# Which PSUM banks the 256-column projections of a two-layer trunk sum in

## The chip, the cores and the metric

The kernel runs on one core of one Trainium2 chip. The metric is the device time of one execution in microseconds (us). The core's engines are TensorE (PE in the profile; its weight loads stand apart as PEld), VectorE (DVE), ScalarE (ACT), GpSimd (POOL) and SyncE (SP, which here only issues DMAs). Every engine works through its own list of instructions in order, and the lists meet by semaphores. PSUM, where TensorE writes its sums, has eight banks of 128 partitions by 512 float32 values in this kernel's layout.

## The reference, cut to what matters

A sequence of 256 tokens of width 1024 passes two layers. Each layer has a mixer and an expert stage (PEER), and each of these ends in a residual sum and a layer norm.

```
proj = h @ w_in                       # one wide projection, split among three groups
y_a  = gelu(rg_gate) * rg_lru(conv(rg_x))            # recurrent group
y_b  = mamba2(z, silu(conv(xbc)), dt)                # state-space group, chunks of 128
y_c  = sliding_window_attention(q, k, v, sinks)      # attention group
mix  = concat(y_a, y_b, y_c) @ w_out
h    = layer_norm(alpha * h + mix)
q    = h @ wq;  scores = q . keys     # 8 heads, top 16 of 2 x 128 keys each
ffn  = sum over chosen experts of gate * gelu(h . u) * v
h    = layer_norm(alpha * h + ffn)
```

The matrix products keep float32 precision: each float32 operand is split into a high and a low part, and three products (high by high, high by low, low by high) are summed.

## The kernel before

**Weights.** All weight blocks (128 by 1024 float32) lie in one list (`items`) in the order of use. A DMA brings a block into one of four raw buffers. ScalarE copies it to `hi` (L119), and VectorE, or GpSimd for the numbers in `on_pool`, subtracts to get `lo` (L120). `hi` and `lo` have three buffers each, so the split of block n+3 waits until TensorE is done with block n. `weights(key)` (lines 123 to 128) asks for a block and starts the split of two more. In a layer's list, blocks 0 to 12 are xBC and dt, 13 to 16 the recurrent input (rgx), 17 to 20 its gate (rgg), 21 to 26 q, k and v; of 13 to 26, GpSimd splits 14, 16 and 18 and VectorE the rest.

**Two kinds of PSUM buffer.** The pool has two names with four banks each:

```
def bank(shape, name="w"):
    return psum.tile(shape, F32, name="w", bufs=4)

def acc_bank():
    return psum.tile([128, 512], F32, name="acc", bufs=4)
```

A tile of a name takes the next of its four buffers, and its first write waits until everything that read or wrote the tile before it in that buffer is done. `acc` serves the 512-column sums: the z projection (two at a time), the output projection (four), the expert stage's up products (one each for a pair of expert blocks) and its down products (four). `w` serves the rest: the transposes of the layer norm (L282), the background products of the mixer and of the routing, and the 256-column projections.

**The 256-column projections** go through `proj_T` (line 336): 24 matmuls of 128 by 128 by 256 columns into one `[128, 256]` tile, with a weight block as the stationary operand and the transposed residual stream `hTh`, `hTl` as the moving one. Each is then copied out by ScalarE (L745 and L761 into `xp`, L769 into `gg`, L777 into `qT`, `kT`, `vT`; L850 in the expert stage). A mixer has 27 of them (12 xBC, 1 dt, 4 rgx, 4 rgg, 6 qkv), an expert stage 8.

**Background work.** What the three groups compute beside the projections is written as generators, of which the mixer takes a step or two after each projection (`bg.step`). After the 12 xBC blocks these are, in the order written: a small product `pc` and transpose `pb` (L465, then mm through L194), four transpose groups `pt` of `xs` (L484), read by two VectorE operations each (L496 into `xdt`, L497 into `y`), the decay sums from `da` (into `odec`, L490), and then state products, gates (`bda`) and attention. Each of them takes `w` banks.

**Order.** Within a layer the order of each engine's list is fixed when the program is built: the framework's planner goes by the order in which the code emits the instructions, by what they need, and by its own estimate of when buffers come free. Only the layer norm (VectorE, ScalarE), the routing (VectorE) and short groups of matmuls have an order written out by hand. The output projection takes 16 blocks; block 4 is the first that needs the attention, block 8 the first that needs the state-space group.

Of the kernel before, what the change touches and what calls it, by code (L numbers as in the profile page):

```python
# [17 lines left out]
SEQ = 256  # L18
# [30 lines left out]
def trunk(ctx, tc, x, wst, ut, vr, pp_d, rb_d, lnrow, bd_d, keys_d, out):  # L49
# [76 lines left out]
    def weights(key, ahead=True):  # L126
        n = index[key]
        pump_split(n)
        if ahead:
            pump_split(n + LOOK)  # L130
        return splits.pop(n)
# [64 lines left out]
# [5 lines that stand above are left out]
# [135 lines left out]
    def proj_T(w, hT, ps, first=False):  # L336
        hi, lo = w
        hTh, hTl = hT
        if first:
            for n, (a, b) in enumerate(((hi, hTh), (lo, hTh), (hi, hTl))):  # L340
                for k in range(KD):
                    mm(ps, a[:, k * 128:(k + 1) * 128], b[:, k, :], n == 0 and k == 0, n == 2 and k == KD - 1)
            return
        for k in range(KD):
            s = slice(k * 128, (k + 1) * 128)
            mm(ps, hi[:, s], hTh[:, k, :], k == 0, False)
            mm(ps, hi[:, s], hTl[:, k, :], False, False)
            mm(ps, lo[:, s], hTh[:, k, :], False, k == KD - 1)
# [46 lines left out]
    def mixer(l, mix, h, hT, pre):  # L395
# [20 lines left out]
        def dt_task(ps):  # L416
            dtT = mix.tile([16, SEQ], F32, name="dtT")
            ACT.activation(dtT, ps[0:16, :], AF.Copy)
            pd = bank([128, 2, 16])
            for tb in range(2):  # L420
                PE.transpose(pd[:, tb, :], dtT[:, tb * 128:(tb + 1) * 128], ident[0:16, 0:16])
            yield
            DVE.tensor_tensor(dt, pd, RB("dtb", l)[:, None, :].to_broadcast([128, 2, 16]), op=OP.add)
            dr = mix.tile([128, 2, 16], F32, name="dt_raw")
            DVE.tensor_copy(dr, dt)
            log1p_exp_neg_abs(mix, dt.rearrange("p a b -> p (a b)"), dr.rearrange("p a b -> p (a b)"), 32, "sp")
            DVE.scalar_tensor_tensor(da, dt, -1.0, av[:, None, :].to_broadcast([128, 2, 16]),
                                     op0=OP.mult, op1=OP.mult)
            ACT.activation(das[:, 0], da, AF.Copy)
            DVE.tensor_tensor(das[:, 1], da, das[:, 0].bitcast(F32), op=OP.subtract)  # L430
            yield
            yield
# [16 lines left out]
        def ssm_conv(blk, xp):  # L449
            conv(xs[:, blk, :], xp, lambda i: P("scw", l, blk * 4 + i))  # L450
            ACT.activation(xs[:, blk, :], xs[:, blk, :], AF.Silu, bias=P("scb", l, blk))
            yield
# [145 lines left out]
        def rg_conv(blk, xp):  # L598
            conv(xc[:, blk, :], xp, lambda i: P("rgw", l, blk * 4 + i), P("rgb", l, blk))
            yield  # L600
# [138 lines left out]

        order = [8, 9, 10, 11, 0, 1, 2, 3, 4, 5, 6, 7]  # L740
        for n, blk in enumerate(order):
            ps = bank([128, SEQ])
            proj_T(weights(("w", l, n if n < 4 else n + 1)), hT, ps, n == 0)
            xp = pads[n % 4]
            ACT.activation(xp[:, 3:3 + SEQ], ps, AF.Copy)  # L745
            bg.add(ssm_conv(blk, xp))
            bg.step(1)
            if n == 3:
                ps = bank([128, SEQ])
                proj_T(weights(("w", l, 4)), hT, ps)  # L750
                dtt = dt_task(ps)
            if n == 4:
                next(dtt)
# [2 lines left out]
        bg.add(ssm_core())  # L756
        n0 = 1 + N_XBC
        for blk in range(4):
            ps = bank([128, SEQ])
            proj_T(weights(("w", l, n0 + blk)), hT, ps)  # L760
            ACT.activation(pads[blk][:, 3:3 + SEQ], ps, AF.Copy)  # L761
            for _ in rg_conv(blk, pads[blk]):
                pass
            bg.step(RX)
        n0 += N_RGX
        for blk in range(4):
            ps = bank([128, SEQ])
            proj_T(weights(("w", l, n0 + blk)), hT, ps)
            ACT.activation(gg[:, blk, :], ps, AF.Copy)  # L769
            bg.step(RA)  # L770
        n0 += N_RGG
        bg2.add(rg_core())
        for i in range(6):
            ps = bank([128, SEQ])
            proj_T(weights(("w", l, n0 + i)), hT, ps)
            dst = qT[:, i, :] if i < 4 else (kT if i == 4 else vT)
            ACT.activation(dst, ps, AF.Copy)  # L777
            bg.step(RA)
            bg2.step(RB2)
# [54 lines left out]
    def peer(l, pool, hT):  # L834
# [10 lines left out]

        qT = view(120, 8).rearrange("p (a b) -> p a b", b=SEQ)
        for hh in range(8):
            ps = bank([128, SEQ])
            proj_T(weights(("w", l, N_IN + N_OUT + hh)), hT, ps, hh == 0)
            ACT.activation(qT[:, hh, :], ps, AF.Copy)  # L850
        scs = [view(104 + 8 * tb, 8).rearrange("p (h i k) -> p h i k", i=2, k=128) for tb in range(2)]

        for tb in range(2):
            for hq in range(2):
                ps = [bank([128, 4, 128]) for _ in range(2)]
# [185 lines left out]
        for jp_ in range(64):  # L1041
            ps = psum.tile([128, 2, SEQ], F32, name="acc", bufs=4)
# [77 lines left out]
    for l in range(DEPTH):  # L1120
        po = mixer(l, mix, h, hT, consts.pop() if consts else None)

        def resid(tb, nh, acc, po=po, h=h):
            cs = slice(nh * 512, (nh + 1) * 512)
            DVE.scalar_tensor_tensor(h[:, tb, cs], h[:, tb, cs], ALPHA, po[tb][nh], op0=OP.mult, op1=OP.add,
                                     accum_out=acc)
        hT = layer_norm(h, mix, resid, (("g1", l), ("b1", l)), h_dram[l], ("w", l, N_IN + N_OUT))
        mixp.__exit__(None, None, None)
        with tc.tile_pool(name=f"peer{l}", bufs=1) as pool:
            po = peer(l, pool, hT)  # L1130
        mixp = tc.tile_pool(name=f"mix{l + 1}", bufs=1)
        mix = mixp.__enter__()
        h = mix.tile([128, 2, D], F32, name="h")

        def resid2(tb, nh, acc, po=po, h=h, l=l):
            cs = slice(nh * 512, (nh + 1) * 512)
            DVE.scalar_tensor_tensor(h[:, tb, cs], rawtile(("h", l, tb))[:, cs], ALPHA * GS, po[tb][nh],
                                     op0=OP.mult, op1=OP.add, accum_out=acc)
            if nh:
                rawdone(("h", l, tb))  # L1140
        last = l == DEPTH - 1
        outs = [out[tb * 128:(tb + 1) * 128, :] for tb in range(2)]
        hT = layer_norm(h, mix, resid2, (("g2", l), ("b2", l)), outs if last else None,
                        None if last else ("w", l + 1, 0), final=last, unit=GS)
# [74 lines left out]
```

## Time and profile before

| | |
|---|---|
| runs shown | 2021.58, 2026.04, 2031.02 us; median 2026.04 |
| profiled execution | 2025.82 us |
| its span in the trace | 2024.0 us |
| mean granted TensorE clock | 0.988 |
| PE busy | 1958.4 us, 97% of the span |
| DVE, ACT, POOL busy | 1471.8 (73%), 1050.0 (52%), 218.1 (11%) |

The span is the time between the first and the last instruction of the trace. Busy is the sum of an engine's instructions without overlaps. The granted clock is a share of TensorE's full 2.4 GHz; 0.50 means 1.2 GHz. The layers' stages by time: mixer of layer 0 from about 18 to 208 us, its expert stage to about 1010, mixer of layer 1 from about 1018 to 1208, its expert stage to about 2014.

### The profile page before, as it was taken

How to read it: one execution, taken by the hardware profiler on the slowest of the kernel's cores; microseconds unless marked ns; L12 is line 12 of the kernel's file. 1: busy time of each engine (PE TensorE's matmuls, PEld its weight loads, DVE VectorE, ACT ScalarE, POOL GpSimd, SP SyncE). 2: the span in 40 equal slices, each digit the busy share in tenths (PEclk: the TensorE clock that was granted, in tenths of full speed). 3: DMA queues.
4: the chain of work that ended last, by engine and by line, in shares of the span. 5: the costliest groups of instructions: out<-in, count | busy, mean ns of one | idle time of the engine just before them, and what ended most of it. 6: DMA issues, size and time to landing. Idle time of an engine off the chain costs nothing. (4 is left out here: it accounts for less than half of the span.)

```text
span 2024.0 us, 33680 instructions
## 1 busy us (share of the span) xinstructions
PE 1958.4 (97%) x13292; PEld 1774.9 (88%) x13292; DVE 1471.8 (73%) x2584; ACT 1050.0 (52%) x1531; POOL 218.1 (11%) x114
## 2 busy tenths in 40 slices
PE   6999899999999999999999999999999999999998
PEld 6887899999999888888788769989999998888886
DVE  8896598677888655555697865996788885555555
ACT  5576454554444544444566754545444444444444
POOL 3100155500000000000011002554000000000000
PEclk9999899999999999999999999999999999999999
DMA  6434454554444656656554245545445446665665
GB/s 208 136 115 156 167 178 157 169 165 157 158 163 160 187 191 195 196 190 196 194 186 134 96 156 181 177 142 176 158 157 164 159 158 191 194 197 188 197 195 169
DMA packets 95919, 344.85 MB, mean 170 GB/s; under 512 B 11680, under 2 KB 11952, under 8 KB 95760
## 3 DMA queue, kind: packets, MB, share of 16 engines
q1 hardware_dynamic: 95552, 342.27, 51.8%
q8 instruction: 104, 1.70, 0.3%
q0 software_dynamic: 208, 0.42, 0.1%
q14 instruction: 55, 0.45, 0.1%
HBM read 339.51 MB, written 3.15 MB: 169 GB/s over the span
## 5 line engine op out<-in xcount | busy, mean ns | idle before, releaser
L119 ACT ACTIVATE hi<-raw 128x1024 fp32r<-128x1024 f32 x630 | 664.5, 1057 | 565.8 <-PE acc L194 290.7
L120 DVE TENSOR_TENSOR lo<-raw,hi 128x1024 fp32r<-128x1024 f32 x550 | 688.5, 1252 | 318.0 <-ACT hi L119 317.9
L194 PE MATMUL acc<-hTh,hi 128*128 128x256 f32 x2048 | 592.7, 289 | 0.0
L194 PE MATMUL acc<-hTh,lo 128*128 128x256 f32 x2048 | 581.5, 284 | 9.8 <-DVE lo L120 6.1
L194 PE MATMUL acc<-hTl,hi 128*128 128x256 f32 x2048 | 580.9, 284 | 0.0
L194 PE MATMUL acc<-hi,hTl 128*128 128x512 f32 x1056 | 412.0, 390 | 0.0
L194 PE MATMUL acc<-lo,hTh 128*128 128x512 f32 x1056 | 411.6, 390 | 0.0
L194 PE MATMUL acc<-hi,hTh 128*128 128x512 f32 x1056 | 411.3, 390 | 0.0
L194 PEld LDWEIGHTS acc<-hTh,lo 128*128 128x128 f32 x2048 | 394.3, 193 | 11.4 <-DVE lo L120 6.7
L194 PEld LDWEIGHTS acc<-hTl,hi 128*128 128x128 f32 x2048 | 394.8, 193 | 0.0
L194 PEld LDWEIGHTS acc<-hTh,hi 128*128 128x128 f32 x2048 | 394.4, 193 | 0.2
L120 POOL TENSOR_TENSOR lo<-raw,hi 128x1024 fp32r<-128x1024 f32 x80 | 203.3, 2545 | 597.1 <-ACT hi L119 543.1
L194 PEld LDWEIGHTS acc<-hi,hTl 128*128 128x128 f32 x1056 | 198.2, 188 | 42.8 <-issue 1.6
L194 PEld LDWEIGHTS acc<-hi,hTh 128*128 128x128 f32 x1056 | 198.2, 188 | 41.7 <-issue 0.7
L194 PEld LDWEIGHTS acc<-lo,hTh 128*128 128x128 f32 x1056 | 198.3, 188 | 40.5
L194 PE MATMUL w<-hTh,hi 128*128 128x256 f32 x560 | 161.7, 299 | 7.6 <-DVE y L497 5.7
L1080 ACT ACTIVATE hTh<-act 128x512 fp32r<-128x512 f32 x124 | 81.1, 659 | 166.2 <-PE acc L194 166.2
L1081 DVE TENSOR_TENSOR hTl<-act,hTh 128x512 fp32r<-128x512 f32 x124 | 85.5, 693 | 100.4 <-ACT hTh L1080 100.4
L194 PE MATMUL w<-hTh,lo 128*128 128x256 f32 x560 | 156.7, 289 | 0.0
L194 PE MATMUL w<-hTl,hi 128*128 128x256 f32 x560 | 155.5, 287 | 0.0
L969 DVE TENSOR_TENSOR eq<-iota,ijT 128x1024 f16<-128x1024 f16 x128 | 88.4, 690 | 53.1 <-PE w L194 52.3
L194 PEld LDWEIGHTS w<-hTh,hi 128*128 128x128 f32 x560 | 109.9, 202 | 9.9 <-issue 6.2
(265 smaller groups left out, 1919.8 us busy)
## 6 DMA issues: line engine op xcount, KB each, us to landing
raw<-in_ut SPq DMA_DIRECT2D x256, 512.0 KB, 3.5
raw<-in_vr SPq DMA_DIRECT2D x256, 512.0 KB, 3.6
raw<-in_wst SPq DMA_DIRECT2D x118, 512.0 KB, 3.5
raw<-in_lnrow SPq DMA_DIRECT2D x8, 512.0 KB, 3.7
hd<-h SPq DMA_DIRECT2D x4, 512.0 KB, 3.9
raw<-hd SPq DMA_DIRECT2D x4, 512.0 KB, 4.2
h<-in_x SPq DMA_DIRECT2D x2, 512.0 KB, 5.7
y<-in_lnrow SPq DMA_DIRECT2D x2, 512.0 KB, 7.0
```

Of the source, the lines that this page charges most:

```text
L119: ACT.activation(hi, raw, AF.Copy)
L120: (POOL if n in on_pool else DVE).tensor_tensor(lo, raw, hi.bitcast(F32), op=OP.subtract)
L194: PE.matmul(ps, lhsT, rhs, start=start, stop=stop)
L969: DVE.tensor_tensor(eq.rearrange("p c a k e -> p (c a) k e"), iota2[:, None, :, :].to_broadcast(sh), pairs(ijT[:, g]), op=OP.is_equal)
L1080: ACT.activation(gh, src, AF.Copy)
L1081: DVE.tensor_tensor(gl, src, gh.bitcast(F32), op=OP.subtract)
```

## The change

Each of the 256-column projections takes an `acc` buffer and uses its first 256 columns. All else is as it was.

```diff
         for n, blk in enumerate(order):
-            ps = bank([128, SEQ])
+            ps = acc_bank()[:, 0:SEQ]
             proj_T(weights(("w", l, n if n < 4 else n + 1)), hT, ps, n == 0)
...
             if n == 3:
-                ps = bank([128, SEQ])
+                ps = acc_bank()[:, 0:SEQ]
                 proj_T(weights(("w", l, 4)), hT, ps)
...
         for blk in range(4):
-            ps = bank([128, SEQ])
+            ps = acc_bank()[:, 0:SEQ]
             proj_T(weights(("w", l, n0 + blk)), hT, ps)
             ACT.activation(pads[blk][:, 3:3 + SEQ], ps, AF.Copy)
...
         for blk in range(4):
-            ps = bank([128, SEQ])
+            ps = acc_bank()[:, 0:SEQ]
             proj_T(weights(("w", l, n0 + blk)), hT, ps)
             ACT.activation(gg[:, blk, :], ps, AF.Copy)
...
         for i in range(6):
-            ps = bank([128, SEQ])
+            ps = acc_bank()[:, 0:SEQ]
             proj_T(weights(("w", l, n0 + i)), hT, ps)
...
         for hh in range(8):
-            ps = bank([128, SEQ])
+            ps = acc_bank()[:, 0:SEQ]
             proj_T(weights(("w", l, N_IN + N_OUT + hh)), hT, ps, hh == 0)
```

## Rows read from the trace of the kernel before

**Rows 1.** The page: busy time of each engine, share of the span, instructions.
```profile
PE 1958.4 (97%) x13292; PEld 1774.9 (88%) x13292; DVE 1471.8 (73%) x2584; ACT 1050.0 (52%) x1531; POOL 218.1 (11%) x114
```
**Rows 2.** Waits of PE: engine, line, waited for; us in total, times, longest us.
```profile
PE w L282 <- DVE h L275: 34.2, 14, 12.2
...
PE w L194 <- DVE y L497: 5.7, 2, 2.9
...
PE w L194 <- ACT xp L761: 1.5, 2, 0.9
...
PE w L194 <- ACT qT L777: 0.3, 2, 0.2
```
**Rows 3.** Windows, layer 0: stretch, us, busy (x) of PE, PEld, DVE, ACT, POOL; PEclk; DMA.
```profile
68.00:92.00 24.00, 20.27 (x157) 19.87 (x156) 20.51 (x30) 9.85 (x17) 2.50 (x1) 0.93 0.44 149
92.00:112.00 20.00, 19.84 (x132) 17.14 (x131) 12.42 (x17) 18.98 (x30) 0.00 (x0) 1.00 0.34 113
112.00:157.00 45.00, 44.68 (x258) 34.91 (x257) 41.33 (x71) 32.73 (x65) 0.00 (x0) 1.00 0.31 104
```
**Rows 4.** Timeline of PE, layer 0: start us, us, what, count, [idle before <- releaser].
```profile
67.52 1.06 PE L194 MATMUL w<-xs 128*128 128x128 f32 x8
69.44 0.39 PE L194 MATMUL w<-hTh,hi 128*128 128x256 f32 x1 [0.86 <-ACT xp L761]
...
79.02 0.60 PE L484 MATMUL w<-ident,xs 128*128 128x128 f32 x4
82.49 0.36 PE L194 MATMUL w<-hTh,hi 128*128 128x256 f32 x1 [2.87 <-DVE y L497]
...
86.88 0.66 PE L484 MATMUL w<-ident,xs 128*128 128x128 f32 x4
87.29 0.36 PE L194 MATMUL w<-hTh,hi 128*128 128x256 f32 x1
...
90.25 0.29 PE L194 MATMUL w<-da,tri_gt 128*128 128x16 f32 x2
```
**Rows 5.** Timeline of DVE, layer 0.
```profile
77.03 1.22 DVE L120 TENSOR_TENSOR lo<-raw,hi 128x1024 fp32r<-128x1024 f32 x1
...
80.53 1.22 DVE L120 TENSOR_TENSOR lo<-raw,hi 128x1024 fp32r<-128x1024 f32 x1
81.66 0.68 DVE L497 TENSOR_TENSOR y<-w,rb 128x512 f32<-128x512 f32 x1
...
84.05 1.21 DVE L120 TENSOR_TENSOR lo<-raw,hi 128x1024 fp32r<-128x1024 f32 x1
...
99.44 1.23 DVE L120 TENSOR_TENSOR lo<-raw,hi 128x1024 fp32r<-128x1024 f32 x1 [5.01 <-ACT hi L119]
```
**Rows 6.** Windows inside the stretch around 82.49 us, columns as in rows 3.
```profile
84.00:85.00 1.00, 1.00 (x7) 1.00 (x7) 1.00 (x2) 0.00 (x0) 0.00 (x0) 0.50 0.37 148
...
87.00:88.00 1.00, 1.00 (x11) 1.00 (x10) 0.42 (x1) 1.00 (x2) 0.00 (x0) 1.00 0.87 352
```
**Rows 7.** Chain that ended last, layer 1: start us, us, what.
```profile
1082.35 4.40 PE w L194 x24
```
**Rows 8.** Timeline of ACT, layer 0.
```profile
69.02 0.36 ACT L761 ACTIVATE xp<-w 128x256 f32<-128x256 f32 x1
...
86.90 1.06 ACT L119 ACTIVATE hi<-raw 128x1024 fp32r<-128x1024 f32 x1 [6.42 <-PE w L194]
```
**Rows 9.** Timeline of DVE, ACT and PE in the layer norm before layer 0.
```profile
14.33 0.68 DVE L289 TENSOR_TENSOR hTl<-w,hTh 128x512 fp32r<-128x512 f32 x1
...
17.25 0.60 ACT L284 ACTIVATE hTh<-w 128x512 fp32r<-128x512 f32 x1 [0.56 <-PE w L282]
...
18.86 1.12 PE L282 MATMUL w<-ident,h 128*128 128x128 f32 x4 [1.64 <-DVE h L275]
```
**Rows 10.** Timeline of PE where output block 4 begins, layer 0.
```profile
172.23 0.65 PE L194 MATMUL w<-pT,vn 128*64 128x256 f32 x4
172.81 0.50 PE L194 MATMUL acc<-hi,yTl 128*128 128x512 f32 x1
```

## The prediction

> **What bounds the kernel now.** The page's first section comes first: PE is busy for 1958.4 of 2024.0 us [rows 1]. So the other engines matter only where they make PE stand, or where PE runs at its low clock, and no change of banks can give back more than the other 66 us and what the clock costs. The list of waits of PE says where those 66 us are [rows 2]. The largest entry, 34.2 us, is the transposes of the layer norm waiting for VectorE to finish h; the edit leaves those in the w banks. Three entries concern the projections (out is w, line 194): 5.7 us for "y L497" in two waits, 1.5 us for "xp L761" in two, 0.3 us for "qT L777" in two. Each occurs once a layer.
>
> The next look is at what these waits are for. A projection reads hi, lo, hTh and hTl; it reads neither y nor xp nor qT. What L497, L761 and L777 have in common is that each is the last reader of a w tile. So these are waits for a bank, not for data. The windows [rows 3] show that they fall into one stretch of each mixer, 68 to 92 us in layer 0, where PE is busy for 20.27 of 24 us and its granted clock is 0.93; in the two stretches after it PE is busy all but 0.16 and 0.32 us. The timeline of PE [rows 4] shows each: the fourth rgx projection begins at 69.44 after 0.86 us of standing, the third rgg projection at 82.49 after 2.87 us, with nothing else of PE's list run meanwhile.
>
> **The change part by part.** No instruction is added or removed: 35 projections per layer write the same 256 columns in another bank, and ScalarE reads them from there. I cost a matmul or a copy in another bank at nothing. What changes is whom a projection waits for.
>
> *The wait at 82.49.* Before, its buffer is that of an xs transpose four w tiles back, whose last reader L497 runs from 81.66 for 0.68 us [rows 5]: 82.34, and the projection starts 0.15 us later. After, its buffer is that of the projection four before it, long copied out. What is late next are its weights. It is block 19; GpSimd splits 16 and 18, so the VectorE splits in order are 19 at 77.03, 20 at 80.53, 21 at 84.05, ended by 78.25, 81.75 and 85.26 [rows 5]. PE's previous work, the transposes at 79.02, ends at 79.62 [rows 4], after 78.25. So all 2.87 us go, in both layers: 5.7 us.
>
> *The wait at 69.44.* Its buffer is freed by the copy at 69.02 to 69.38 [rows 8], which ScalarE reaches late. After, the four acc banks hold only rgx projections here, and the one it needs was copied out earlier still; its weights (block 16, GpSimd) must be there, for the matmul runs as soon as the bank is free. It can follow the products that end at 68.58 [rows 4]: 0.86 us in layer 0 and, from the total of 1.5, some 0.65 in layer 1 [rows 2]. With the third wait, 0.3 us in both layers, 1.8 us.
>
> *The clock.* Behind the long wait the granted clock is 0.50, which is 1.2 GHz, and by 87 it is 1.00 again [rows 6]; before it PE had stood for 2.87 us. The 24 matmuls from 82.49 to 86.88 take 4.39 us; the next 24, from 87.29 to 90.25, take 2.96 [rows 4]. That is 1.43 us, and layer 1 shows the same 4.40 us [rows 7]. Without the standing there is no reason for the fall: 2.9 us for both layers. The Trainium skill ("TensorE: Matmul & The Clock Gate", Part 1) calls the ramp under 1% of a typical span and advises against fitting it. By that the sum would be 7.5 us instead of 10.4. The rows decide for counting it: 2.9 us is 0.14% of the span, but over a quarter of this gain.
>
> *What is late next.* The gain is 0.86 + 2.87 + 1.43 + 0.16 = 5.3 us a layer at most, 5.2 of it before the q projections. The first of these, block 21, starts now behind the decay sums, at 90.25 + 0.29 = 90.54 [rows 4], and would then at 90.54 - 5.16 = 85.38; its lo is there at 85.26 if VectorE keeps its order. That is a margin of 0.1 us. Its cost if gone is one VectorE operation of 0.68 or 1.22 us a layer. The next split waited for PE anyway: ScalarE stood 6.42 us before 86.90 until TensorE had released the buffer [rows 8], so it moves with PE. Behind it VectorE stands 5.01 us before 99.44 [rows 5], enough to take up a shift of 5 us. ScalarE is full from 92 to 112 (18.98 of 20 us, rows 3), but its chain there hangs on the last rgg projection and the decay sums, which move too. DMA is at 0.34 to 0.44 of its time in these stretches [rows 3]. So I expect the shift to reach the end of the mixer.
>
> *Parts worth nothing.* The 13 xBC and dt projections: PE waits for none of them. The 8 of the expert stage: likewise; the sums of the output projection that hold acc are read at the start of the layer norm. The first projection after a layer norm may now get a bank before the transposes' low parts are formed. In layer 0 a bank is free from 15.0 (14.33 + 0.68) and four matmuls' inputs from 17.85 (17.25 + 0.60), yet the transposes at 18.86 still go first [rows 9]; so I take 0. As bound: four matmuls, at most as long as the 1.12 us of the four transposes there, in each of three such places, 3.4 us of gain. z and the output sums: the acc tiles ahead of them are projections that ScalarE has copied out; bound by the longest such wait of the trace, 0.86 us a layer, 1.7 us of loss.
>
> **The sum.** 5.7 + 1.8 + 2.9 = 10.4 us; I take off 0.6 us, half an operation of 0.68 a layer for the thin margin at block 21. The profiled execution took 2025.82 us, 1.8 more than its span and 0.2 less than the median of the runs shown: 2025.8 - 9.8 = **2016.0 us**, 0.5% below the median. A measurement of this kernel can tell about 0.5% from no change, so the forecast lies on that line.
>
> **The rivals.**
>
> *The gain ends at the attention.* Output block 4 starts at 172.81, straight behind the last attention product at 172.23 to 172.88 [rows 10]: by then PE has used up all output work that doesn't need the attention. From 112 to 157 VectorE is busy for 41.33 of 45 us [rows 3]. If the attention's chain is held by VectorE and doesn't move, PE comes 5.3 us earlier and waits 5.3 us there. Then 2025.8. For it: no slack at block 4. Against it: VectorE's pause of 5.01 us, which lets the chain start earlier.
>
> *The wait stays, under another name.* The list of PE is in order. If the planner now puts the decay sums, whose bank is that of the first transpose group, ahead of the third rgg projection, they wait for the same L497 and everything behind them too; only the waits of 0.86 and 0.16 go: 2025.8 - 1.8 = 2024. The Trainium skill ("PSUM — Partial Sum Buffer", Engine vs sequencer instructions) says that matmuls start and complete in program order; the trace agrees, for nothing overtook the projection in its 2.87 us. Against it: in the code the decay sums are emitted behind the fourth rgg projection, and PE runs them there [rows 4].
>
> *Slower: the background falls behind.* With no bank to hold them, the planner may run projections ahead of background products that are not ready in its estimate. Each projection put ahead delays the chain to the attention by some 3.0 us, while PE's other work comes 5.3 us earlier and runs out at block 4. With n projections ahead the end of a mixer moves by 3.0 n - 5.3 us, plus 1.43 for the clock. It decides from n = 2 (0.7 + 1.4 a layer, 2030 us); at n = 3 it is 2036. For it: the order is planned anew. Against it: the code emits one background step or two behind each projection, and at 79.02, 86.88 and 90.25 PE follows that.
>
> **How the numbers follow.** The forecast has a chance of 0.62, with its own range of 2010 to 2021: down by the 3.4 us of the layer norm and some 3 us (one projection) that a new order of the list may bring, up by 1.7 us for z and 1.22 in place of 0.3 us at block 21 in each layer. The attention rival has 0.14, the renamed wait 0.10, the slower one 0.14. Within the forecast I hold 0.38 for more than 0.5% and 0.24 for less. The first two rivals add 0.02 to faster and 0.22 to no change, the slower one 0.01 and 0.13. That gives 0.40, 0.47 and 0.13. The range of 2008 to 2031 takes in the first two rivals and the slower one at n = 2.
>
> **What would show it.** Right: in the waits of PE the entries for y L497, xp L761 and qT L777 are gone; the third rgg projection follows its transposes directly; no window of the mixer behind 23 us (1023 in layer 1) has a clock of 0.50; the mixers are some 5 us shorter each and the expert stages are not. Wrong: a wait of some 5 us before output block 4, a wait of PE for lo in the q projections, a decay sum ahead of the rgg projections, or expert stages that differ by more than 3 us.

## The result and the profile after

The changed kernel takes 2015.09 us (median of 8 runs, 2009.91 to 2017.31) and the kernel before 2027.56 us (8 runs, 2021.58 to 2031.07). The ratio is 0.9935, with a 95% interval of 0.9923 to 0.9947, so the gain is 13 us, between 11 and 16. The forecast of 2016.0 us was right in time and in sign; the gain that it counted on, 9.8 us, lies just under that interval. The profiled execution took 2014.87 us and has a span of 2013.1 us, 10.9 less than before.

The page of the kernel after answers to [rows 1]. PE's busy time fell by 4.4 us and its idle time (span less busy) from 65.6 to 59.1, by 6.5; the two make up the 10.9.

```profile
span 2013.1 us, 33664 instructions
PE 1954.0 (97%) x13292; PEld 1773.6 (88%) x13292; DVE 1474.9 (73%) x2584; ACT 1049.3 (52%) x1531; POOL 218.6 (11%) x114
```

The waits of PE after (engine, line, waited for; us in total, times, longest) are the whole list:

```profile
PE w L282 <- DVE h L275: 34.7, 15, 12.2
PE acc L194 <- DVE lo L120: 8.0, 4, 2.1
PE w L194 <- DVE act L941: 4.1, 2, 2.1
PE acc L194 <- POOL lo L120: 2.2, 5, 0.7
PE w L714 <- DVE at_small L685: 0.4, 2, 0.2
```

Against [rows 2], the three entries for y L497, xp L761 and qT L777 (5.7 + 1.5 + 0.3 us) are gone and no new name has come in their place. The layer norm's entry stands at 34.7 (34.2 before). What is left are waits for data: h, lo, act and at_small are operands of the matmuls that wait for them. The two entries for lo stood at 6.1 and 3.7 us before; together they hardly moved (9.8 and 10.2).

The timeline of PE in layer 0 after (start us, us, what) answers to [rows 4] and [rows 10]:

```profile
67.80 1.06 PE L194 MATMUL w<-xs 128*128 128x128 f32 x8
...
68.61 0.36 PE L194 MATMUL acc<-hTh,hi 128*128 128x256 f32 x1
...
78.18 0.60 PE L484 MATMUL w<-ident,xs 128*128 128x128 f32 x4
78.53 0.36 PE L194 MATMUL acc<-hTh,hi 128*128 128x256 f32 x1
...
81.49 0.60 PE L484 MATMUL w<-ident,xs 128*128 128x128 f32 x4
...
84.80 0.29 PE L194 MATMUL w<-da,tri_gt 128*128 128x16 f32 x2
85.17 0.36 PE L194 MATMUL acc<-hTh,hi 128*128 128x256 f32 x1
...
166.55 0.65 PE L194 MATMUL w<-pT,vn 128*64 128x256 f32 x4
167.13 0.50 PE L194 MATMUL acc<-hi,yTl 128*128 128x512 f32 x1
```

The order of PE's list is that of before (in the whole trace, one matmul behind each of three layer norms has moved); the output names changed from w to acc. Read it from start to start. From the transposes to the third rgg projection it was 3.47 us (79.02 to 82.49) and is 0.35. The 24 matmuls of that projection ran to the next transposes in 4.39 us (82.49 to 86.88) and now in 2.96 (78.53 to 81.49). From the products on xs to the fourth rgx projection it was 1.92 us and is 0.81. Output block 4, where the attention ends, begins at 167.13, which was 172.81: 5.68 us earlier, and still with no wait before it.

The clock behind the long wait, as windows of the same five us in both layers (stretch, us, busy of PE, PEld, DVE, ACT, POOL, granted clock, DMA). Before:

```profile
83.00:88.00 5.00, 5.00 (x32) 5.00 (x31) 3.29 (x5) 1.10 (x2) 0.00 (x0) 0.66 0.55 194
1083.00:1088.00 5.00, 5.00 (x32) 5.00 (x31) 3.27 (x5) 1.33 (x2) 0.00 (x0) 0.66 0.56 193
```

After:

```profile
83.00:88.00 5.00, 5.00 (x43) 4.85 (x42) 5.00 (x8) 3.07 (x5) 0.00 (x0) 1.00 0.61 198
1083.00:1088.00 5.00, 5.00 (x41) 4.89 (x41) 4.62 (x6) 4.94 (x9) 0.00 (x0) 1.00 0.72 220
```

PE is busy for all 5 us in all four rows, yet it gets 32 matmuls done in the one kernel and 41 to 43 in the other: at a clock of 0.66 (a part of the stretch at 1.2 GHz) "busy" is worth less. This loss is in no list of waits.

The windows after that answer to [rows 3]:

```profile
68.00:92.00 24.00, 24.00 (x200) 23.74 (x199) 22.34 (x32) 15.49 (x24) 2.52 (x1) 1.00 0.51 161
92.00:112.00 20.00, 19.96 (x132) 17.18 (x132) 16.18 (x23) 19.11 (x34) 0.00 (x0) 1.00 0.36 124
112.00:157.00 45.00, 44.72 (x248) 34.19 (x248) 39.50 (x73) 31.64 (x67) 0.00 (x0) 1.00 0.31 106
```

The first stretch now holds 200 matmuls of PE where it held 157, with no standing and at the full clock. The second is as full of ScalarE as before, 19.11 of 20 us.

The stages, from the start of one layer norm's last transposes to the next (the last to the end of the span), from the timelines of both kernels:

| us | mixer 0 | expert stage 0 | mixer 1 | expert stage 1 |
|---|---|---|---|---|
| before | 198.14 | 801.69 | 198.75 | 806.56 |
| after | 192.09 | 805.30 | 192.51 | 804.36 |
| difference | -6.05 | +3.61 | -6.24 | -2.20 |

The mixers gave 12.3 us; the expert stages, in which the sums go on as before, took back 1.4 on balance.

### The profile page after: what moved, and what is told of

It reads as the page before. It is cut to its first block, busy times and chain, and to the rows that moved or that the text cites. A ratio compares the mean times of both kernels' runs of the same rounds, so it can differ in the third digit from the quotient of the medians.

```text
span 2013.1 us, 33664 instructions
## 1 busy us (share of the span) xinstructions
PE 1954.0 (97%) x13292; PEld 1773.6 (88%) x13292; DVE 1474.9 (73%) x2584; ACT 1049.3 (52%) x1531; POOL 218.6 (11%) x114
## 4 chain that ended last, share of the span: by engine, by line
PE 88%; DVE 9%; ACT 2%; issue 1%; DMA 0%; POOL 0%; SPq 0%; DVEq 0%; ACTq 0%; POOLq 0%
PE acc L194 81%; PE w L194 6%; DVE lo L120 2%; DVE h L275 1%; DVE act L867 1%; DVE act L868 1%; DVE act L870 1%; DVE act L937 1%; DVE act L869 1%; ACT hi L119 0%; DMA h<-in_x 0%; DVE act L866 0%; ACT probs L688 0%; DVE sz L259 0%; DVE act L923 0%
## 5 line engine op out<-in xcount | busy, mean ns | idle before, releaser
L194 PE MATMUL acc<-hTh,hi 128*128 128x256 f32 x2608 | 754.6, 292 | 0.0
L194 PE MATMUL acc<-hTh,lo 128*128 128x256 f32 x2608 | 739.4, 285 | 10.2 <-DVE lo L120 8.0
L194 PE MATMUL acc<-hTl,hi 128*128 128x256 f32 x2608 | 736.5, 284 | 0.0
L194 PEld LDWEIGHTS acc<-hTh,lo 128*128 128x128 f32 x2608 | 503.2, 194 | 12.2 <-DVE lo L120 8.8
L194 PEld LDWEIGHTS acc<-hTh,hi 128*128 128x128 f32 x2608 | 504.6, 195 | 0.6
L194 PEld LDWEIGHTS acc<-hTl,hi 128*128 128x128 f32 x2608 | 502.0, 193 | 0.3
L1015 ACT ACTIVATE act<-acc 128x512 f32<-128x512 f32 (+38 forms) x126 | 61.8, 491 | 89.2 <-DVE act L1013 89.1
L971 DVE TENSOR_TENSOR ga<-eq,gT 128x1024 f16<-128x1024 f16 x128 | 90.1, 704 | 0.0
L194 PE MATMUL w<-eq,ga 128*128 128x128 f16 x1024 | 81.2, 220 | 0.0
L989 DVE TENSOR_TENSOR act<-act,w 128x224 f32<-128x224 f32 (+34 forms) x128 | 67.2, 525 | 6.2 <-ACT act L1015 5.6
```

What stands on the lines that cost most here:

```text
L194: PE.matmul(ps, lhsT, rhs, start=start, stop=stop)
L971: DVE.tensor_tensor(A.rearrange("p c a k e -> p c (a k) e"), eq[:, 0].rearrange("p a k e -> p (a k) e")[:, None].to_broadcast([128, 2, TG ...
L989: DVE.tensor_tensor(v[:, :, 0:c], v[:, :, 0:c], g[:, :, 0:c], op=OP.mult)
L1015: ACT.activation(a[:, :, t:SEQ], ps[:, :, t:SEQ], AF.Gelu)
```

## The experiments

All ratios are against the kernel before, run on the same chip in the same job. A gain in us is one minus the ratio, times the median of before. Where a kernel has "extra" matmuls, these form sums that nobody reads.

**Which projections matter.** The change was split in two: the 27 projections of the mixers alone, and the 8 of the expert stages alone.

```diff
 e1: the five `ps = bank([128, SEQ])` of the mixer
 e2: the one of the expert stage
-            ps = bank([128, SEQ])
+            ps = acc_bank()[:, 0:SEQ]
```

> The mixer's 27 projections of a layer sum in acc as after the change, the 8 of the expert stage in w as before. Bank theory (a projection stands because its w bank is still being read by L497, L761 or L777, all in the mixer): all of the gain, some 12 us below before, mixers as long as after the change (192 us from the last layer-norm transposes to the next). Rival (each projection gains a little from the move itself): 27 of 35 of it, some 9.5 us.

> Only the 8 projections of the expert stage sum in acc. Bank theory: no change (within 2 us of before); the waits of PE for y L497 (5.7 us in 2), xp L761 (1.5) and qT L777 (0.3) stay, and so do the low clock behind the long one and mixers of 198 us. The expert stages' lengths move by some us either way as they did between before and after, by how often the clock falls behind VectorE waits there. Rival (each projection gains from the move): 8 of 35, some 2.8 us faster.

The mixer part: 2016.06 us, ratio 0.993 (0.9916 to 0.9943). The expert part: 2028.34 us, ratio 0.9998 (0.9989 to 1.0007). The first can't be told from the whole gain and the second not from nothing. The rival, a little for each projection, is out: its 9.5 and 2.8 us lie outside the two intervals (11.6 to 17.0 us and -1.4 to 2.2). The waits for L497, L761 and L777 stand in the trace of the second unchanged (5.7, 1.5 and 0.3 us).

**Which wait matters.** Only the four rgg projections of each layer in acc:

```diff
         for blk in range(4):
-            ps = bank([128, SEQ])
+            ps = acc_bank()[:, 0:SEQ]
             proj_T(weights(("w", l, n0 + blk)), hT, ps)
             ACT.activation(gg[:, blk, :], ps, AF.Copy)
```

> Only the 4 rgg projections of each layer sum in acc. Bank theory: the long wait goes, that is 2.87 us of standing, 0.25 us between the modelled end of a matmul and the start that would follow it, and 1.43 us of clock, 4.55 us a layer: 9.1 us below before; the wait for xp L761 of 0.7 to 0.9 us a layer stays. Rival (each projection gains a little): 4 of 35 of 12 us, 1.4 us.

2018.88 us, ratio 0.9959 (0.9945 to 0.9972), a gain of 8.3 us. Of the waits of PE, that for L497 is gone and the two small ones stay:

```profile
PE w L194 <- ACT xp L761: 1.5, 2, 0.8
...
PE w L194 <- ACT qT L777: 0.3, 2, 0.2
```

So the one long wait of each layer carries about two thirds of the gain (8.3 of 13.2 us); the sum had 5.7 + 2.9 of 10.4.

**Is it acc, or the queue behind the transposes?** The projections stay in w, and the four groups of xs transposes go to acc instead:

```diff
-                    pt = bank([128, 4, 128])
+                    pt = psum.tile([128, 4, 128], F32, name="acc", bufs=4)
```

> The other way round: all projections stay in w, and only the four groups of xs transposes (L484) of a mixer go to acc. Bank theory: the projections no longer stand behind the readers of these transposes, so the wait for L497 goes and its clock loss with it, 4.55 us a layer, 9.1 us below before, as with the gate projections alone; xp L761 stays. Rival (what helps is that projections sum in acc): no gain.

2018.41 us, ratio 0.9949 (0.9935 to 0.9962), a gain of 10.3 us where 9.1 were expected. The waits of PE again have no L497 and keep the small ones:

```profile
PE w L194 <- ACT xp L761: 1.5, 2, 0.8
...
PE w L194 <- ACT qT L777: 0.3, 2, 0.2
```

The projection needs no better bank. It must only not take the buffer that L497 still reads, and either of the two can be moved to bring that about.

**Filling the wait.** The kernel before, with 20 extra matmuls of 256 columns just ahead of the third rgg projection, so that PE works where it stood:

```diff
             bg.step(RA)
+            if blk == 1:
+                fill = acc_bank()
+                for k in range(20):
+                    mm(fill[:, 0:SEQ], hTh[:, k % KD, 0:128], hTh[:, k % KD, :], True, True)
```

> As before the change, with 20 extra matmuls (256 columns, into an acc tile that nobody reads) ahead of the third rgg projection: 20 x 0.12 = 2.4 us of the 2.87 us of standing are filled, and nothing of the wait itself is taken away. Clock theory: PE's standing shrinks to about 0.5 us, the granted clock stays at 1.00 and the 24 matmuls behind it take 3.0 us in place of 4.4: 1.43 us a layer, 2.9 us below before. Rival (the low clock there is not due to the standing, or costs nothing on the whole): no gain, or a loss of up to 0.5 us.

The timeline of PE in layer 0 shows what was meant:

```profile
79.65 0.60 PE L484 MATMUL w<-ident,xs 128*128 128x128 f32 x4
80.00 2.63 PE L194 MATMUL acc<-hTh 128*128 128x256 f32 x20
83.10 0.35 PE L194 MATMUL w<-hTh,hi 128*128 128x256 f32 x1 [0.47 <-DVE y L497]
...
86.04 0.60 PE L484 MATMUL w<-ident,xs 128*128 128x128 f32 x4
```

From the transposes to the projection it is still 3.45 us (79.65 to 83.10): the buffer comes no earlier. But the 24 matmuls behind take 2.94 us (83.10 to 86.04) instead of 4.39, and the clock of 84 to 86 us is 1.00. So the 1.43 us a layer hang on the standing, and are had back without touching the wait. In layer 1 it is the same with 18 of the 20 matmuls; two ran early, at 1021 us. In all, though, it took 2019.41 us, ratio 0.9966 (0.9953 to 0.998): 6.9 us of gain where the expectation had 2.9. The other 4 us were not gained at the wait. Each of the ten executions had a mean clock of 0.990 to 0.992; the kernel before had 0.985 to 0.990 beside them. Call the clock's loss the sum, over windows of 1 us, of PE's busy time multiplied by one minus the granted clock: it is 17.5 us in the profile of before and 11.6 in this one, 5.9 less, of which 3.4 lie at the wait (1.7 a layer). It is an upper measure: a fall can also fill time in which PE would else stand, as shown further down.

**Is that extra gain the filling's?** The same kernel with 10 extra matmuls more, ahead of the fourth rgg projection:

```diff
+            if blk in (1, 2):
+                fill = acc_bank()
+                for k in range(20 if blk == 1 else 10):
...
```

> The filled wait (20 extra matmuls ahead of the third rgg projection, which still stands for its w bank), and 10 more ahead of the fourth, where PE has no pause: the later work lies 1.2 us a layer later than in the filled wait, and nothing else differs. By the local sum 2.4 us above the filled wait, some 2022. If the 4 to 5 us by which the filled wait beat its local sum came from where its later stands happened to lie in time, they need not come again: up to 2026. If they come with filling the wait, they stay: 2022.

2027.5 us, ratio 0.9993 (0.9982 to 1.0004): not the filled wait's time and 2.4 us more, some 2022, but the other branch, up to 2026, and a little over it. Counted from the kernel before, the local terms are 2.9 us less for the clock and 2.4 more for the added work, 0.5 less in all; the ratio says 1.4 less, between 3.6 less and 0.8 more, so it fits. The waits of PE for banks are those of the kernel above (L497 at 1.2 us in two, down from 5.7). Its twelve executions lie in two groups: five from 2019.0 to 2023.4 us with a mean clock of 0.990 to 0.992, seven from 2027.3 to 2028.9 with 0.988 to 0.989. The clock's loss in its profile is 17.1 us. So the 2.9 us stand, and the 4 us above them did not come again: they went with clock falls elsewhere, most of them in the expert stages. What decides those falls was not found.

**The change again, and with work added.** In one job the changed kernel was run again; in another it was run with 10 and with 20 of the extra matmuls (the edit of the filled wait, on the changed kernel). As each adds 0.12 us to the start of the next, the local price is 2.4 and 4.8 us for both layers.

```diff
-                for k in range(20):
+                for k in range(10):
```

> The kernel after the change once more, beside the two others on the same chip: 12 to 13 us below before. Its mixers again take 192 us; by the theory that the clock falls behind VectorE waits of 2 us in the expert stage in some executions and not in others, its expert stages differ from those of the first profile (805.3 and 804.4 us) by some us, without a change in the waits.

> As after the change, with 10 extra matmuls of 256 columns (into an acc tile that nobody reads) ahead of the third rgg projection of each layer, where PE now has no pause. Local theory: 10 x 0.12 = 1.2 us a layer and no more, 2.4 us above the kernel after, that is 9 to 10 us below before. If the number of falls of the clock elsewhere depends on where in time the stands of PE lie, the shift of 1.2 us a layer moves the mean granted clock and the time by some us more, either way.

> The same with 20 extra matmuls, the filler of the filled wait, but without the wait: local theory 4.8 us above the kernel after, some 2020 us. The filled wait came out 5 us faster than its local sum; if the extra matmuls themselves bring those 5 us, this one is no slower than the kernel after; if it was where they put the later stands in time, this one keeps most of its 4.8 us or moves by some us either way with the granted clock.

The change again: 2015.44 us, ratio 0.9947 (0.9927 to 0.9967). With 10: 2013.04, 0.9934 (0.992 to 0.9948). With 20: 2015.21, 0.9948 (0.9934 to 0.9962). Against the change's own 0.9935 and 0.9947 neither price can be seen in the total: with 10 the ratio is no higher, and with 20 it lies level with the higher of the two. That is a miss of the local sum by 2 to 5 us, of the same size as the scatter above and hardly more than the intervals allow (some 2.8 us either way). In the 20's five executions it shows again: three at 2013.8 to 2015.2 us with a clock of 0.990 to 0.991, two at 2019.5 and 2019.8 with 0.989.

**Can the layer norm's standing be used?** With the first projection in acc, its first four matmuls can run ahead of the last transposes of the layer norm, if PE's order is written out there:

```diff
+            if (tb, c) == (1, 1):
+                begin_T(splits[nxt], hTh)
...
+    def begin_T(w, hTh):
+        ps = acc_bank()[:, 0:SEQ]
+        for k in range(4):
+            mm(ps, w[0][:, k * 128:(k + 1) * 128], hTh[:, k, :], k == 0, False)
+        begun.append(ps)
...
```

> As after the change, and the first four matmuls of the first projection behind each layer norm are placed ahead of the last group of the layer norm's transposes, which they could not be while the four w banks held transposes. They fill some 0.9 us of the standing of 1.7 us there, in three layer norms: 2.7 us below the kernel after. Rival (VectorE's last operation of the layer norm is the bound and the four matmuls only move from a time of low clock to another): less than 1 us.

2019.25 us, ratio 0.9962 (0.9949 to 0.9974); 3.8 us over the changed kernel of the same job instead of 2.7 under it. The windows of the second layer norm show what went with it. The changed kernel, in its first profile:

```profile
204.00:212.00 8.00, 3.42 (x17) 2.66 (x18) 7.63 (x14) 4.27 (x8) 4.18 (x2) 0.70 0.43 148
212.00:220.00 8.00, 8.00 (x62) 8.00 (x61) 3.72 (x4) 4.17 (x6) 1.02 (x1) 0.88 0.91 326
```

With the early matmuls:

```profile
204.00:212.00 8.00, 4.37 (x17) 3.17 (x18) 7.34 (x13) 4.87 (x8) 3.12 (x2) 0.55 0.34 131
212.00:220.00 8.00, 7.60 (x40) 7.16 (x40) 3.53 (x6) 2.67 (x4) 2.01 (x1) 0.59 0.90 324
```

The layer norms' standing did shrink (the waits for h are 27.0 us in its list, 34.7 in that of the change), but the clock stays low for longer: 40 matmuls instead of 62 in the second 8 us. New waits come too (for hTh 2.7 us, and for GpSimd's lo 6.2 us in place of 2.2), since the matmuls need inputs that are just being made. The list of PE differs in more than the four matmuls, too: others of the first projection, on hTl and lo, also moved ahead. Which of these began it was not told apart.

**Extra matmuls in the layer norm's standing.** Instead of the projection's own, matmuls on data that is long there, ahead of the transpose groups of the layer norms: 8, 0, 7 and 6 of them in one kernel (the 8 of 128 columns, the others of 512), 4, 0, 4 and 3 in the other. PE's order in these layer norms is written out by hand here too; by its trace, the half filling has PE's order of the changed kernel with the extra matmuls put in and nothing else moved, while in the full filling matmuls of the first projection moved as well.

```diff
+                for j in range((4, 0, 4, 3)[tb * 2 + c]):
+                    if tb == 0:
+                        mm(fills[0][:, 0:128], ident, h[:, 1, 512 + j % 4 * 128:640 + j % 4 * 128], True, True)
+                    else:
+                        mm(fills[0], identb, mask0.rearrange("p a b -> p (a b)"), True, True)
             ps = bank([128, 4, 128])
```

> As after the change, with PE kept busy in the layer norms behind a matmul stage: extra matmuls whose sums nobody reads, 8 small ones (128 columns) ahead of the first transposes, 7 and 6 of 512 columns ahead of the third and fourth group. Clock theory: PE does not fall to 0.50 there, which cost 2.1, 2.2 and 3.2 us in the three layer norms of the first profile after the change, and the transposes take 0.63 us in place of 1.1: some 7 us below the kernel after, 19 below before. Rival (VectorE's chain through the layer norm is the bound, or the fillers are late and hold the transposes): no gain, or slower by up to 2 us.

> The same with half the fillers (4, then 4 and 3), which leave PE some 1 us of standing ahead of each group: by the clock theory a part of the 7 us, by the rival none; if the full fillers are late and this one is not, it is the faster of the two.

The full filling: 2014.11 us, ratio 0.9936 (0.9923 to 0.995), not better than the change alone. Half of it: 2010.98 us (2010.12 to 2013.55), ratio 0.992 (0.9906 to 0.9933), the lowest median of all versions. Its windows of the same layer norm, one us later:

```profile
205.00:213.00 8.00, 4.65 (x28) 2.99 (x29) 7.63 (x14) 4.74 (x10) 4.42 (x2) 1.00 0.49 149
213.00:221.00 8.00, 8.00 (x67) 8.00 (x68) 4.54 (x5) 3.49 (x5) 0.79 (x1) 1.00 0.97 362
```

The clock is 1.00 through both; in the third layer norm it fell once, at 1014 us. The mean clock is 0.994 to 0.997 in its five executions. The full filling holds it as well (0.995 to 0.997) but gives the gain back. Why is open: its profile fell on its fastest execution (2010.68 us), and of the new waits in its list (1.7 us for hTl, 1.6 and 0.8 for h) those for h stand in the half filling's list too. Against the changed kernel the half filling is 3 us ahead by the ratios (0.992 and 0.9935), 5.5 by those of the repeat. The two were not run in one job and their intervals overlap, so this gain is likely, not settled.

**The stretch by itself.** The total scatters, but the stretch in which the waits lie does not. Read from the timelines of PE, it goes from the L465 transposes to the third group of gates' products (`w<-xc,bda`, behind the third q projection; 67.31 to 104.05 us in layer 0 before):

| kernel | layer 0, us | layer 1, us |
|---|---|---|
| before; expert part alone | 36.7; 36.7 | 36.5; 36.5 |
| the change; again; mixer part alone | 30.8; 30.8; 30.8 | 30.6; 30.6; 30.6 |
| only rgg in acc | 32.1 | 31.9 |
| only the transposes in acc | 32.1 | 32.0 |
| filled wait; with 10 more | 35.2; 36.4 | 35.0; 36.2 |
| the change with 10; with 20 | 31.8; 33.0 | 31.8; 33.0 |

Here every local price comes out: 4.6 us a layer for the long wait with its clock, by either cure (4.55 expected); 1.5 for the clock alone (1.43); 1.2 for 10 extra matmuls beside the filled wait, 1.0 to 1.2 for 10 and 2.2 to 2.4 for 20 in the changed kernel. So the misses of the totals arise outside the stretch.

## Why the prediction was right

**The mechanism held.** The third rgg projection waited for a buffer and not for data; moving either user away removes the wait (the gate-only and the transpose kernels). The waits vanish from the list, PE's order is kept, and nothing of the gain is lost before the attention.

**The size of the waits was too small.** The sum took each wait as the trace prints it, from the modelled end of the work before. But matmuls that follow each other start before that end: the transposes at 78.18 for 0.60 us end at 78.78, and the projection starts at 78.53, 0.25 us earlier. So the long wait cost 3.12 us (3.47 less 0.35) and not 2.87; that at 69.44 cost 1.11 (1.92 less 0.81) and not 0.86. The q projections' wait gave some 0.4 in place of 0.16. With six waits, this term is 1.5 us short.

**The clock's term held.** 4.39 less 2.96 us is 1.43 a layer, as forecast, in both layers, and the filled wait shows that it hangs on the standing. The Trainium skill ("TensorE: Matmul & The Clock Gate", Part 1) advises against fitting the ramp, under 1% of a span, and calls the number of slow matmuls variable from run to run of one kernel. For the total this case agrees: the clock's loss is 17.5 us of 2024 before and 14.3 of 2013 after, and the two groups of the shifted filling show the scatter. For the fall behind this wait, which stands at the same place in both layers of both kernels that keep the wait whole (before and the expert part alone), counting it was right: its 2.9 us are nearly a quarter of the mixers' gain. After the change no window of either mixer is below 1.00, as the prediction asked.

**The thin margin cost less.** Block 21 was taken to come out 0.1 us behind its lo, with 0.6 us taken off for the risk. VectorE's splits after, in layer 0, with the one that is late next:

```profile
77.29 1.22 DVE L120 TENSOR_TENSOR lo<-raw,hi 128x1024 fp32r<-128x1024 f32 x1
...
80.79 1.22 DVE L120 TENSOR_TENSOR lo<-raw,hi 128x1024 fp32r<-128x1024 f32 x1
...
84.32 1.22 DVE L120 TENSOR_TENSOR lo<-raw,hi 128x1024 fp32r<-128x1024 f32 x1
...
93.98 1.23 DVE L120 TENSOR_TENSOR lo<-raw,hi 128x1024 fp32r<-128x1024 f32 x1 [3.25 <-ACT hi L119]
```

The third ends at 85.54. The projection began at 85.17, earlier than the 85.38 of the sum, since 5.45 us were gained ahead of it (before, it began at 90.62: the sum had left out the second of two groups of decay sums); and its third matmul, the first that reads lo, came at 85.59. So it gave way by 0.2 us in layer 0 (3.16 us for its 24 matmuls in place of 2.95) and by none in layer 1. So a wait of PE for lo in the q projections, one of the signs of being wrong, did appear, at a fifth of a us. The split that is late next moved from 99.44 to 93.98, and the idle time before it shrank from 5.01 to 3.25 us: the pause took up 1.8 of the 5.5 us, for VectorE's work ahead of it came 3.7 us earlier by itself.

The terms together: the stretch of the table above went from 36.74 to 30.80 us in layer 0 and from 36.54 to 30.59 in layer 1. That is 11.9 us, where the forecast had 10.4 and took 0.6 off. The part of layer 0 is 1.11 + 3.12 + 1.43 + 0.4 less 0.2, or 5.9.

**Parts worth nothing** were worth nothing: the expert stage's eight (0.9998), and the rest of the mixer can't be told from nothing: the mixer part's 14.2 us, less the gate-only kernel's 8.3, less 3.0 for the small waits (1.11 + 0.4 in two layers), leave 2.9 us, with an uncertainty of 3.8 from the two intervals. The timelines are sharper: behind the stretch, up to the first transposes of the next layer norm, layer 0 takes 106.04 us before and 106.03 after, layer 1 107.02 and 106.96; ahead of it, from the layer norm's last transposes, 48.45 and 48.74, 48.68 and 48.44.

**The rivals.** The attention rival is refuted by block 4 at 167.13, 5.68 us earlier and with no wait: VectorE did not hold the chain, which moved with the rest. The renamed wait is refuted by the decay sums at 84.80, behind the fourth rgg projection, and by the list of waits. The slower rival needed two projections ahead of the background; PE's order, the same as before in this stretch, has none.

**One marker was badly chosen.** Expert stages that differ by more than 3 us were to show the prediction wrong; that of layer 0 grew by 3.6. PE stands for about 2 us three times in each expert stage, and the clock falls behind some of these stands and not behind others. The stands of layer 0 before, from the timeline of PE:

```profile
319.34 0.39 PE L194 MATMUL acc<-hTh,lo 128*128 128x256 f32 x1 [2.10 <-DVE lo L120]
...
328.02 0.39 PE L194 MATMUL acc<-hTh,lo 128*128 128x256 f32 x1 [1.71 <-POOL lo L120]
...
384.28 0.40 PE L194 MATMUL w<-identb,act 128*128 128x128 bf16 x4 [1.87 <-DVE act L941]
```

After, with a shorter one at 321.63:

```profile
312.93 0.58 PE L194 MATMUL acc<-hTh,lo 128*128 128x256 f32 x1 [2.10 <-DVE lo L120]
...
321.63 0.39 PE L194 MATMUL acc<-hTh,lo 128*128 128x256 f32 x1 [0.24 <-POOL lo L120]
...
335.32 0.39 PE L194 MATMUL acc<-hTh,lo 128*128 128x256 f32 x1 [1.92 <-DVE lo L120]
...
380.30 0.40 PE L194 MATMUL w<-identb,act 128*128 128x128 bf16 x4 [2.04 <-DVE act L941]
```

The windows of 10 us there (columns as above) show the clock. Before:

```profile
310.00:320.00 10.00, 7.90 (x66) 7.70 (x65) 9.72 (x20) 2.64 (x3) 4.86 (x2) 1.00 0.34 107
...
330.00:340.00 10.00, 10.00 (x75) 10.00 (x75) 9.52 (x32) 3.70 (x4) 4.85 (x3) 0.86 0.61 204
380.00:390.00 10.00, 8.13 (x77) 7.93 (x76) 7.67 (x12) 5.15 (x6) 3.12 (x2) 1.00 0.34 107
```

After:

```profile
310.00:320.00 10.00, 7.91 (x53) 7.69 (x52) 8.72 (x26) 4.25 (x4) 2.61 (x2) 0.83 0.32 105
...
330.00:340.00 10.00, 8.08 (x61) 7.78 (x60) 9.55 (x28) 3.61 (x4) 6.06 (x2) 0.84 0.45 153
380.00:390.00 10.00, 9.70 (x85) 9.66 (x86) 4.14 (x5) 6.00 (x7) 5.42 (x2) 0.83 0.34 107
```

Before, the clock fell behind one of the three stands of layer 0 (the second), after behind all three; in layer 1 it was the reverse, two falls before and one after. Nor is each fall a loss of time. From the end of the first stand to the end of the wait for GpSimd's lo it is 8.68 us before, with the clock up and 1.71 us of standing, and 8.70 us after, with the clock down and 0.24. The mixer kernel, whose expert stages are as before, had 806.00 and 806.16 us for its two, in layer 0 4.3 us more than before, so 3 us is within what an unchanged stage shows and is no sign of the change.

**What was luck.** The gain was 13.2 us where 9.8 were forecast. That the total came so near the forecast all the same (2015.09 for 2016.0) has two grounds that the sum knew nothing of: the sum was taken from a profile of 2025.82 us, 1.7 below the median of before in the result, and in the profiles the expert stages took 1.4 us back while the mixers gave 2.5 more than the sum.

## What to carry to other kernels

Where the engine that bounds a kernel waits for an instruction whose output it does not read, look for a shared pool of buffers: the slow reader of another tile, some places back in the rotation, is holding it; here moving either user to another pool cured it. Measure such a wait from start to start against a place that has none, and count the matmuls behind it at the lower clock as part of its cost. Prove a term of 1 or 2 us by windows and timelines at its place, since the total moves by several us with clock falls far away that the edit only shifts.

## What the runs showed that was not expected

Behind standing of about 2 us the clock falls to 1.2 GHz in some places and not in others of one execution (of 310 to 320, 330 to 340 and 380 to 390 us in one before and in three after), though PE's list there is the same and the stands are nearly as long. Behind the first stand of an expert stage a fall cost no time, since the next wait was shorter by as much. Executions of one kernel differ too: those of the shifted filling spread over 9.9 us, the shorter ones at the higher mean clock. What decides it stays open.

Work that nobody needs may pay. Eleven extra matmuls in each of three layer norms raised the mean clock from 0.988 to 0.991 up to 0.994 to 0.997 and went with the lowest time, 2010.98 us, while twice as many gave nothing over the change, and real matmuls moved there, which had to wait for their inputs, cost 3.8 us.
